# First two channel tiles of a GLU projected from unnormalized rows, the RMSNorm factor applied to their results

## The chip, the cores and the metric

The program runs on one core of a Trainium2 chip. The metric is the device time of one execution in microseconds. A core has a matrix engine (TensorE, here PE, with its weight loads PEld), a vector engine (VectorE, DVE), a scalar engine (ScalarE, ACT), a general one (GpSimd, POOL) and an engine that here only issues transfers (SyncE, SP). Each executes its own instructions strictly in order and waits on semaphores for the others.

## The reference, cut

One inference step of a streaming encoder: a Conformer convolution module, a SwiGLU feed-forward layer, a shared key and value projection, an attention layer with another feed-forward, a final norm. The change lies in the first projection of the convolution module.

```python
def rms_norm(x, g):
    xf = x.astype(jnp.float32)
    y = xf * lax.rsqrt(jnp.mean(xf * xf, axis=-1, keepdims=True) + EPS)
    return (y * g.astype(jnp.float32)).astype(x.dtype)

def conv_module(h, hist, g, w_pw1, b_pw1, w_dw, b_dw, ln_g, ln_b, w_pw2, b_pw2):
    a, gate = jnp.split(rms_norm(h, g) @ w_pw1 + b_pw1, 2, axis=-1)
    glu = a * jax.nn.sigmoid(gate)
    full = jnp.concatenate([hist.astype(glu.dtype), glu], axis=1)
    y = lax.conv_general_dilated(
        full, w_dw[:, None, :].astype(full.dtype), window_strides=(1,), padding="VALID",
        dimension_numbers=("NWC", "WIO", "NWC"), feature_group_count=D_MODEL) + b_dw
    y = jax.nn.silu(layer_norm(y, ln_g, ln_b))
    return h + y @ w_pw2 + b_pw2, full[:, -CONV_HIST:]
```

The model width is 1024; there are 512 prompt rows and 8 x 16 sample rows, 640 in all. Everything is float32.

## The kernel before

Channels lie on the 128 partitions, rows (frames) on the free axis, so the width is 8 slices k of 128 channels. The 640 rows are two halves g of 320 columns: half 0 has the 128 sample rows and 192 prompt rows, half 1 the other 320 prompt rows. `h` holds x of all rows.

**Exact products.** A float32 matmul is made of three cheaper ones: each operand is split into a high part and a remainder, x into `xh` and `xl`, a weight tile `raw` into `whi` and `wlo`, and `mm3` (L199) adds whi·xh, wlo·xh and whi·xl (L202, L203, L204) into one PSUM buffer. The high part is a copy on ACT to a rounding type (L178 for weights, L190 for rows), the remainder a subtraction on DVE (L183, L192). A weight tile of one channel tile c is 128 x 2048: both sides of the GLU (value and gate), 8 slices each. Two of `raw`, `whi` and `wlo` exist at a time; a third must wait for the first one's last use.

**The norm.** `rms` (L298) squares the 8 slices of a half (ACT L211, some DVE L214), adds the squares (L233), sums over the partitions with three small matmuls against a constant (L243), adds epsilon (`rst`, L280), takes the power -0.5 on POOL (L287), and spreads the result over the partitions with three matmuls (L257), so that the factor of each row lies in PSUM. Then for each slice DVE computes n = h · gain · factor (L309), ACT xh and DVE xl.

**The GLU.** `glu(c, g)` multiplies half g with weight tile c: 2 sides x 8 slices x 3 = 48 matmuls of 320 columns into two PSUM buffers out of four. ACT turns them into tanh (L814) and a scaled copy (L817), DVE multiplies these into `gall` (the gate: L823 for sample rows, L830 for prompt rows).

**The depthwise convolution** has 31 taps. They are shared out: DVE accumulates some channel tiles in PSUM (L866 starts one, L869 adds a tap, 512 prompt columns or 128 sample columns); POOL accumulates the prompt rows of c=0 and c=3 (`conv_pool`: ACT scales a shifted view into one of four buffers `cvt`, L876, POOL adds it to `ca`, L879); PE does the others with small diagonal matrices `w4` (L923), which POOL builds (`conv_load`, L890) from the tap weights `dwv`; three w4 buffers exist. All tiles end in `y` (L838), on which a LayerNorm follows, whose sums are again matmuls (L243).

**The order.** `PLAN` lists the steps: a c is glu(c, 0), b c is glu(c, 1), x is glu(1, 0) with the norm of half 1 put between its two sides (argument `mid`), y loads half 1 of x, later letters do further tiles and the convolution. A scheduling layer orders the instructions of each engine by priority: work in a `high_priority` block goes ahead of what was written earlier, `behind` and `issue_after` tie an instruction behind a given one. Transfers go through SP's queue in the order in which they are written: half 0 of x, weight tiles 0 and 1 in quarters, history, half 1 of x; ACT's queue takes the small vectors and `dwv`. While nothing is there to multiply, PE multiplies the identity (`warm`, L149), 30, 9 and 5 times at three places.

Half 1's norm borrows two w4 buffers for its first n (argument `hold`), so the second and third w4 are built after those n are used up.

Of the kernel before, what the change touches and what calls it, by code (L numbers as in the profile page):

```python
# [47 lines left out]
PL1 = (0, 2, 0, 0, 0, 0, 0, 0)  # L48
# [7 lines left out]
SSQ = 'avavavaa'  # L56
# [29 lines left out]
def tile_trunk(ctx, tc, xT, vecs, hist, w_pw1, w_pw2, w_in0, w_out0, w_os0, w_in1, w_out1, w_os1,  # L86
# [65 lines left out]
    def wsplit(src, k, n, parts=1, pool=0, cuts=1, gains=None, late=False, ties=()):  # L152
        raw = wp.tile([P, 2048], F32, tag="raw", name=nm("raw"))
# [18 lines left out]
        def split():  # L172
            with tc.high_priority(offset=HP):
                for i in range(cuts):
# [5 lines left out]
                    for eng, a, b in ((nc.vector, a, c), (nc.gpsimd, c, b)):  # L180
                        if a < b:
                            with behind(*tie):
                                eng.tensor_tensor(out=lo[:, a:b], in0=raw[:, a:b],  # L183
                                                  in1=hi[:, a:b].bitcast(F32), op=ALU.subtract)
# [37 lines left out]
    def colmean(st, pieces, n, cut, tag, eng=nc.gpsimd, accp=None, late=(KT, None)):  # L222
# [17 lines left out]
        for k, f in enumerate(srcs):  # L240
            s = f()
            for t, a in enumerate(tiles(n)):
                mean_end[0] = nc.tensor.matmul(st[:, 512 + t * w + k:513 + t * w + k], s[:, a:a + P],  # L243
                                               onec, start=True, stop=True).ins
# [53 lines left out]
    def rms(g, gain, engs=SQ, cut=CUT, eng=nc.gpsimd, hold=None, hook=None):  # L298
        n = gr[g][1]
        bc, _ = rstd_bc([hp(g, k) for k in range(KT)], n, engs, cut, None, eng,  # L300
                        accp=hold and hold(), hook=hook)
# [4 lines left out]
        for k in range(KT):
            t = hold() if hold and k < 2 else tp.tile([P, tw[0]], F32, tag="n1", name=nm("n1"),
                                                       bufs=NB1)
            norm_end["n"].append(nc.vector.scalar_tensor_tensor(  # L309
                out=t[:, :n], in0=hp(g, k), scalar=col(gain, k), in1=bc, op0=ALU.mult,  # L310
                op1=ALU.mult).ins)
# [458 lines left out]
    def first():  # L770
        with behind(mean_end[0]):
            warm(WARM[1])
        pws[0] = wsplit(w_pw1[0], 16, P, cuts=4, pool=PL1[0],
                        ties=[(norm_end["sq"], norm_end[e]) for e in ("acc", "acc", "rst", "rst")])

    with tc.issue_after(warm(WARM[0])), tc.high_priority(offset=2 * HP):
        xs = [rms(0, V_NCONV, SSQ, SCUT, nc.vector, hook=first), None]
    pws[1] = wsplit(w_pw1[1], 16, P, cuts=4, pool=PL1[1],
                    ties=(norm_end["sq"], norm_end["n"][3], norm_end["pow"]))
# [13 lines left out]

    def glu_(c, g, wh, wl, mid):
        n = gr[g][1]
        ps = []
        for ab in range(2):
            pt = mmt()
            def some(ks):
                return mm3(pt[:, :n], [(wh[:, (ab * 8 + k) * P:(ab * 8 + k + 1) * P],  # L800
                                        wl[:, (ab * 8 + k) * P:(ab * 8 + k + 1) * P])
                                       for k in ks], xk(xs[g], ks), ks[0] == 0, ks[-1] == KT - 1)

            if mid and ab:
                mid(lambda: some(range(0, 4)).ins)
                with tc.issue_after(norm_spread[0]):
                    some(range(4, KT))
            else:
                some(range(KT))
            ps.append(pt[:, :n])  # L810
        with tc.high_priority(offset=HP):
            cover.clear()
            t = tp.tile([P, tw[0]], F32, tag="t1", name=nm("t1"))
            glu_end[0] = nc.scalar.activation(out=t[:, :n], in_=ps[1], func=AF.Tanh, scale=0.5,  # L814
                                              bias=hb1[:, KT + c:KT + c + 1]).ins
            a = tp.tile([P, tw[0]], F32, tag="t2", name=nm("t2"))
# [1060 lines left out]
```

## Time and profile before

| | |
|---|---|
| median of 3 runs | 1432.19 us (1431.23 to 1434.5) |
| profiled execution | 1431.78 us |
| its span in the trace | 1430.0 us |
| granted TensorE clock | 1.000 |
| busy: PE, DVE, ACT, POOL | 99%, 78%, 52%, 19% of the span |

The profile is of one execution; its time is 1.78 us over its span, since what lies around the span is not in the trace. Times in the trace count from the span's start. A row of the timeline has start, length, engine, line, operation, output and inputs (buffer numbers left out), a count of equal instructions that follow each other, and, in brackets, how long the engine had been idle and what released it. A row of the groups has line, engine, operation, shape and count, then the busy time in us and the mean of one in ns, then the idle time before them. A row of the stretches has the stretch, its length, and for each engine the busy time and count, then the granted clock, the share of the transfer engines and GB/s.

### The profile page before, as it was taken

How to read it: one execution, taken by the hardware profiler on the slowest of the kernel's cores; microseconds unless marked ns; L12 is line 12 of the kernel's file. 1: busy time of each engine (PE TensorE's matmuls, PEld its weight loads, DVE VectorE, ACT ScalarE, POOL GpSimd, SP SyncE). 2: the span in 40 equal slices, each digit the busy share in tenths (PEclk: the TensorE clock that was granted, in tenths of full speed). 3: DMA queues.
4: the chain of work that ended last, by engine and by line, in shares of the span. 5: the costliest groups of instructions: out<-in, count | busy, mean ns of one | idle time of the engine just before them, and what ended most of it. 6: DMA issues, size and time to landing. Idle time of an engine off the chain costs nothing.

```text
span 1430.0 us, 28700 instructions
## 1 busy us (share of the span) xinstructions
PE 1416.8 (99%) x11076; PEld 1364.0 (95%) x11076; DVE 1113.5 (78%) x2490; ACT 746.9 (52%) x1633; POOL 278.4 (19%) x335
## 2 busy tenths in 40 slices
PE   9999999999999999999999999999999999999998
PEld 9998799999999999999998998888999999999998
DVE  7799867898888888765666757667898798798765
ACT  5666554554653554545654554544564564464453
POOL 5699121011111110112111111110011111111101
PEclk9999999999999999999999999999999999999999
DMA  7267424154644644524456555561244544554522
GB/s 248 91 176 187 123 84 143 32 122 122 169 107 121 148 115 117 139 89 174 165 185 205 187 179 173 181 218 51 60 108 118 147 125 110 145 131 109 135 72 74
DMA packets 93722, 192.62 MB, mean 135 GB/s; under 512 B 15121, under 2 KB 45585, under 8 KB 90129
## 3 DMA queue, kind: packets, MB, share of 16 engines
q1 hardware_dynamic: 79216, 160.59, 36.0%
q0 software_dynamic: 13504, 29.37, 10.5%
q8 instruction: 87, 1.43, 0.4%
q10 hardware_dynamic: 864, 0.83, 0.2%
q14 instruction: 51, 0.41, 0.1%
HBM read 179.14 MB, written 11.61 MB: 133 GB/s over the span
## 4 chain that ended last, share of the span: by engine, by line
PE 93%; DVE 4%; ACT 1%; issue 1%; DMA 1%; POOL 0%; DVEq 0%; ACTq 0%; POOLq 0%
PE mm L451 52%; PE mm L1311 11%; PE mm L202 6%; PE mm L204 6%; PE mm L203 6%; PE mm L923 3%; PE w L1311 2%; PE am L1484 1%; PE am L1556 1%; PE am L1500 1%; PE w L1455 1%; PE w L1518 1%; PE w L243 1%; PE mm L149 1%; PE w L257 1%
## 5 line engine op out<-in xcount | busy, mean ns | idle before, releaser
L451 PE MATMUL mm<-XH,whi 128*128 128x320 f32 x896 | 275.9, 310 | 1.0 <-ACT t L463 0.7
L451 PE MATMUL mm<-XH,wlo 128*128 128x320 f32 x896 | 276.2, 309 | 0.0
L451 PE MATMUL mm<-XL,whi 128*128 128x320 f32 x896 | 274.7, 309 | 0.0
L375 ACT ACTIVATE whi<-raw 128x512 fp32r<-128x512 f32 (+2 forms) x280 | 167.5, 613 | 148.4 <-PE mm L451 91.9
L376 DVE TENSOR_TENSOR wlo<-raw,whi 128x512 fp32r<-128x512 f32 (+2 forms) x280 | 183.8, 667 | 29.8 <-ACT whi L375 29.2
L451 PE MATMUL mm<-hid,whi 128*128 128x320 f32 x732 | 170.9, 310 | 0.0
L451 PEld LDWEIGHTS mm<-XH,whi 128*128 128x128 f32 x896 | 167.7, 188 | 2.8 <-ACT t L463 1.5
L451 PEld LDWEIGHTS mm<-XH,wlo 128*128 128x128 f32 x896 | 168.2, 188 | 0.0
L451 PEld LDWEIGHTS mm<-XL,whi 128*128 128x128 f32 x896 | 167.7, 188 | 0.0
L202 PE MATMUL mm<-xh,whi 128*128 128x320 f32 (+2 forms) x416 | 128.8, 312 | 0.5 <-DVE h L733 0.4
L203 PE MATMUL mm<-xh,wlo 128*128 128x320 f32 (+2 forms) x416 | 128.0, 309 | 0.0
L204 PE MATMUL mm<-xl,whi 128*128 128x320 f32 (+2 forms) x416 | 125.5, 310 | 1.0 <-DVE xl L192 1.0
L451 PEld LDWEIGHTS mm<-hid,whi 128*128 128x128 f32 x732 | 124.8, 188 | 1.5 <-DVE h L602 0.9
L451 PE MATMUL mm<-hid,wlo 128*128 128x320 f32 x366 | 113.0, 309 | 0.0
L451 PE MATMUL mm<-XH,shi 128*128 128x320 f32 x344 | 106.2, 310 | 1.2 <-DVE h L1588 0.7
L451 PE MATMUL mm<-XH,slo 128*128 128x320 f32 x344 | 106.0, 308 | 0.0
L602 DVE TENSOR_TENSOR h<-h,mm 128x320 f32<-128x320 f32 x168 | 79.1, 482 | 34.2 <-PE mm L451 34.2
L451 PE MATMUL mm<-XL,shi 128*128 128x320 f32 x344 | 105.6, 308 | 0.0
L375 ACT ACTIVATE shi<-raw 128x512 fp32r<-128x512 f32 (+1 forms) x114 | 66.4, 588 | 59.6 <-PE mm L451 31.6
L879 POOL TENSOR_TENSOR ca<-ca,cvt 128x512 f32<-128x512 f32 x60 | 89.5, 1492 | 17.3 <-ACT cvt L876 11.1
L428 POOL DMA_DIRECT2D s<-in_w_in x38 | 22.0, 578 | 309.1 <-ACT shi L375 67.3
L376 DVE TENSOR_TENSOR slo<-raw,shi 128x512 fp32r<-128x512 f32 (+1 forms) x114 | 72.0, 636 | 12.4 <-ACT shi L375 12.0
(337 smaller groups left out, 3663.1 us busy)
## 6 DMA issues: line engine op xcount, KB each, us to landing
raw<-in_w_in SPq DMA_DIRECT2D x152, 256.0 KB
s<-in_w_in POOLq DMA_DIRECT2D x76, 256.0 KB, 4.3
raw<-in_w_os SPq DMA_DIRECT2D x96, 192.0 KB
cache<-in_ck SPq DMA_DIRECT2D x32, 512.0 KB
cache<-in_cv SPq DMA_DIRECT2D x32, 512.0 KB
raw<-in_w_pw SPq DMA_DIRECT2D x11, 1024.0 KB
s<-in_w_os POOLq DMA_DIRECT2D x48, 192.0 KB, 3.6
raw<-in_w_kq SPq DMA_DIRECT2D x8, 1024.0 KB
```

The costliest lines, as they stand in the source:

```text
L149: end = nc.tensor.matmul(pt[:, 0:P], ident, ident, start=True, stop=True)
L202: nc.tensor.matmul(ps, wh, xh, start=(first and i == 0), stop=False)
L203: nc.tensor.matmul(ps, wl, xh, start=False, stop=False)
L204: end = nc.tensor.matmul(ps, wh, xl, start=False, stop=(stop and i == last))
L375: put_end[1] = nc.scalar.activation(out=hi, in_=src, func=AF.Copy).ins
L376: put_end[0] = nc.vector.tensor_tensor(out=lo, in0=src, in1=hi.bitcast(F32), op=sub).ins
L428: nc.gpsimd.dma_start(s1, src[:, 2 * n:3 * n])
L451: last = nc.tensor.matmul(pt, wt, v, start=(first and k == i == 0), stop=(k == n - 1 and i == 2), skip_group_check=True)
L602: hadd[i, u] = [nc.vector.tensor_tensor(out=hv, in0=hv, in1=pt, op=sub if row else add).ins]
L879: nc.gpsimd.tensor_tensor(out=acc, in0=acc, in1=pr, op=ALU.add)
L923: conv_end[0] = nc.tensor.matmul(pt[32 * q:32 * q + 32, 0:n], w4[0:r, 4 * tg + q, :], mv, start=(tg == 0), stop=(tg == 7)).ins
L1311: step_end[0] = nc.tensor.matmul(ps, w, x, start=i == j == 0, stop=i == len(wts) - 1 and j == 2).ins
```

## The change

The first two channel tiles, c=0 and c=1, are projected from rows that carry the gain but not the norm's factor; since that factor belongs to a row and not to a channel, it can be multiplied onto the 320 columns of the projection's result. The other six tiles use the normalized rows as before, which overwrite the raw ones in the same buffers.

- New function `rows`: for each slice, ACT makes xh = h · gain (rounded), DVE xl = h · gain - xh. It stands for both halves, before any norm.
- `half_rstd` computes the factor as before, and ACT copies it from PSUM to an SBUF tile `bc`, kept in `bch[g]`.
- In `glu_`, for c < 2, DVE multiplies each of the two PSUM results with `bch[g]` into the tiles t1 and t2 before ACT takes tanh and copy from there. These evictions are held back (list `evicts`) until the factor of their half exists.
- `rescale` makes n, xh and xl of all 8 slices again, n now with `bch[g]` from SBUF, into the same `xh`, `xl`.
- The loads interleave x and the quarters of the first weight tile (`ARRIVE`), then the second weight tile, half 1 of x, and `dwv`, which moves from ACT's queue to SP's.
- All squares are taken on ACT (three were on DVE), all remainders of weight tile 1 on DVE (POOL had four pieces of 256 columns).
- The first 30 warm-up products become 19, the other two places have none.
- The order of the plan: glu(0,0), then glu(1,0) with half 0's norm between (x), glu(0,1) with half 1's norm between (z), the rescale of half 0 (r0), glu(1,1), the rescale of half 1 (r1). Within c < 2 the products go by half of the slices, so that they can start with slices 0 to 3.
- The w4 builds are tied behind the latest power; ACT's conversions for POOL's taps of c=0 are tied, two rows apart, behind the xh of the rescale.

```diff
+AT = 2, 2
+ARRIVE = "x0 x1 w0 w2 x2 x3 w1 w3".split()
...
-PL1 = (0, 2, 0, 0, 0, 0, 0, 0)
+PL1 = (0, 0, 0, 0, 0, 0, 0, 0)
...
-SSQ = 'avavavaa'
+SSQ = 'aaaaaaaa'
...
-WARM = 30, 9, 5, 0
+WARM = 19
...
-PLAN = ("a0 y x1 b0 b1 q0 dp1s0 c2 ds1p2 D3 C4 S3 q3 C5 E6 u S4 A4 F6 u k ds2 B4 E7 e S5 A5 F7 f k k k S6 A6 "
+PLAN = ("a0 x1 z0 r0 b1 r1 q0 dp1s0 c2 ds1p2 D3 C4 S3 q3 C5 E6 u S4 A4 F6 u k ds2 B4 E7 e S5 A5 F7 f k k k S6 A6 "
...
+    def rows(g, gain, ks, x):
+        for k in ks:
+            with tc.high_priority(offset=HP):
+                nc.scalar.activation(out=x[0][:, k, :], in_=hp(g, k), func=AF.Copy,
+                                     scale=col(gain, k))
+                nc.vector.scalar_tensor_tensor(out=x[1][:, k, :], in0=hp(g, k),
+                                               scalar=col(gain, k),
+                                               in1=x[0][:, k, :].bitcast(F32), op0=ALU.mult,
+                                               op1=ALU.subtract)
+
+    def half_rstd(g, engs, eng, hook, late=(KT, None)):
         n = gr[g][1]
...
+        b = xp.tile([P, n], F32, tag=f"bc{g}", name=nm("bc"))
+        with tc.high_priority(offset=HP):
+            nc.scalar.activation(out=b, in_=bc, func=AF.Copy)
+        return b
+
+    def rescale(g, gain, x):
+        n = gr[g][1]
         for k in range(KT):
...
+            t = tp.tile([P, tw[0]], F32, tag=sqt[0], name=nm("n"))
+            nc.vector.scalar_tensor_tensor(out=t[:, :n], in0=hp(g, k), scalar=col(gain, k),
+                                           in1=bch[g], op0=ALU.mult, op1=ALU.mult)
+            norm_end["rows"] = xsplit(t[:, :n], x[0][:, k, :], x[1][:, k, :]).ins
...
+        if c < 2:
+            parts = [(ab, range(4 * u, 4 * u + 4)) for u in range(2) for ab in range(2)]
+        else:
+            parts = [(ab, range(KT)) for ab in range(2)]
...
+                if c < 2:
+                    av, bv = a[:, :n], t[:, :n]
+                    nc.vector.tensor_tensor(out=av, in0=pts[0], in1=bch[g], op=ALU.mult)
+                    nc.vector.tensor_tensor(out=bv, in0=pts[1], in1=bch[g], op=ALU.mult)
...
+            with behind(*(norm_end["xh"][min(2 * j - 9, -1):][:1] if j > 1 and c == 0 else ())):
+                nc.scalar.activation(out=pr, in_=taps(c, 1, j), func=AF.Identity, scale=wj,
+                                     **({} if j else {"bias": col(V_BDW, c)}))
...
     def conv_load(c):
         w4 = w4t().rearrange("p (a b) -> p a b", a=32)
...
+        with behind(norm_end["pow"]):
...
-            pws[c + 1] = wsplit(w_pw1[c + 1], 16, P)
+            pws[c + 1] = wsplit(w_pw1[c + 1], 16, P, ties=(norm_end["rows"], norm_end["xh"][-1]))
...
+            if g == 0:
+                glu(1, 0, *pws[1], mid=(AT[0], mid))
+                rows(1, V_NCONV, range(KT), xs[1])
+            else:
+                glu(0, 1, *pws[0], mid=(AT[1], mid))
+                pws[2] = wsplit(w_pw1[2], 16, P, pool=PL1[2], cuts=2)
+        elif op == "r":
+            with tc.high_priority(offset=HP * c), behind(*[norm_end["lo"]][:c]):
+                rescale(c, V_NCONV, xs[c])
```

Two places on DVE's queue matter. The first is what follows the `rst` of half 1 (a row has line, operation, output and inputs with their numbers, and shape). Before, two gates and the rows of half 1, whose factor is `w_39` in PSUM:

```order
L280 TENSOR_SCALAR rst_373<-w_39_346 128x3
L823 SCALAR_TENSOR_TENSOR gall<-t_34_308,t_35_310 128x8x16
L830 SCALAR_TENSOR_TENSOR gall<-t_34_308,t_35_310 128x192
L309 SCALAR_TENSOR_TENSOR w_52_394<-h,vec,w_39_346 128x320
L309 SCALAR_TENSOR_TENSOR w_53_398<-h,vec,w_39_346 128x320
L309 SCALAR_TENSOR_TENSOR n_54_402<-h,vec,w_39_346 128x320
L309 SCALAR_TENSOR_TENSOR n_55_406<-h,vec,w_39_346 128x320
L192 TENSOR_TENSOR xl_393<-w_52_394,xh_392 128x320
```

Now it is the second half of half 0's rescale, with its factor `bc_305` in SBUF; then the evictions of glu(0, 1) with half 1's factor `bc_426`, and the remainder of c=2's weight tile:

```order
L292 TENSOR_SCALAR rst_407<-w_35_379 128x3
L203 TENSOR_TENSOR xl_112<-n_468,xh_111 128x320
L333 SCALAR_TENSOR_TENSOR n_476<-h,vec,bc_305 128x320
L203 TENSOR_TENSOR xl_112<-n_472,xh_111 128x320
L333 SCALAR_TENSOR_TENSOR n_480<-h,vec,bc_305 128x320
L203 TENSOR_TENSOR xl_112<-n_476,xh_111 128x320
L333 SCALAR_TENSOR_TENSOR n_484<-h,vec,bc_305 128x320
L203 TENSOR_TENSOR xl_112<-n_480,xh_111 128x320
L203 TENSOR_TENSOR xl_112<-n_484,xh_111 128x320
L862 TENSOR_TENSOR t_49_441<-mm_353,bc_426 128x320
L863 TENSOR_TENSOR t_48_440<-mm_354,bc_426 128x320
L193 TENSOR_TENSOR wlo_449<-raw_447,whi_448 128x1024 x2
```

So the rows stand behind the `rst` of the other half, and POOL's power and its three w4 builds, which follow on POOL's queue, run beside them.

The second place is ahead of the remainder of c=3's weight tile (2048 columns in one piece). Before, DVE went from c=2's remainder over a gate and the first taps to it:

```order
L183 TENSOR_TENSOR wlo_714<-raw_712,whi_713 128x1024 x2
L830 SCALAR_TENSOR_TENSOR gall<-t_68_550,t_69_552 128x320
L866 TENSOR_SCALAR w_101_649<-gall,dwv,vec 128x512
L866 TENSOR_SCALAR w_116_840<-gall,dwv,vec 128x128
L866 TENSOR_SCALAR w_101_649<-gall,dwv,vec 128x128
L183 TENSOR_TENSOR wlo_723<-raw_721,whi_722 128x2048
```

Now 30 rows stand between the two remainders: the evictions of glu(1, 1), two gates, the rescale of half 1, and taps between its rows. The last of them:

```order
L333 SCALAR_TENSOR_TENSOR n_569<-h,vec,bc_426 128x320
L203 TENSOR_TENSOR xl_114<-n_565,xh_113 128x320
L918 SCALAR_TENSOR_TENSOR w_104_671<-gall,dwv,w_104_671 128x512
L333 SCALAR_TENSOR_TENSOR n_573<-h,vec,bc_426 128x320
L203 TENSOR_TENSOR xl_114<-n_569,xh_113 128x320
L918 SCALAR_TENSOR_TENSOR w_104_671<-gall,dwv,w_104_671 128x128
L203 TENSOR_TENSOR xl_114<-n_573,xh_113 128x320
L918 SCALAR_TENSOR_TENSOR w_104_671<-gall,dwv,w_104_671 128x512
L918 SCALAR_TENSOR_TENSOR w_104_671<-gall,dwv,w_104_671 128x128
L918 SCALAR_TENSOR_TENSOR w_104_671<-gall,dwv,w_104_671 128x512
L193 TENSOR_TENSOR wlo_736<-raw_734,whi_735 128x2048
```

The same rows on ACT and POOL follow: the conversions for POOL's taps of c=0 stand one after every second xh of that rescale.

More of the change, by code (lines that the diff above doesn't have):

```diff
@@ L150, in warm, with wsplit @@
         return end.ins
-    def wsplit(src, k, n, parts=1, pool=0, cuts=1, gains=None, late=False, ties=()):
-        raw = wp.tile([P, 2048], F32, tag="raw", name=nm("raw"))
+    def wsplit(src, k, n, parts=1, pool=0, cuts=1, gains=None, late=False, ties=(), raw=None, order=None):
+        loaded = raw is not None
+        raw = raw or wp.tile([P, 2048], F32, tag="raw", name=nm("raw"))
         hi = wp.tile([P, 2048], F32R, tag="whi", name=nm("whi"))
@@ L156, in wsplit @@
         sz = k * n
-        if parts > 1:
+        if loaded:
+            pass
+        elif parts > 1:
             nc.sync.dma_start(raw[:, :sz].rearrange("p (m c) -> p m c", m=parts), src)
@@ L162, in wsplit @@
                 a, b = sz * i // cuts, sz * (i + 1) // cuts
-                with behind(norm_end["x"]) if cuts > 2 else nullcontext():
-                    nc.sync.dma_start(raw[:, a:b], src[:, a:b])
+                nc.sync.dma_start(raw[:, a:b], src[:, a:b])
         if gains is not None:
@@ L171, in wsplit, with split @@
             return hi, lo
-        def split():
+        def split(only=None):
             with tc.high_priority(offset=HP):
-                for i in range(cuts):
+                for i in range(cuts) if only is None else (only,):
                     a, b = sz * i // cuts, sz * (i + 1) // cuts
@@ L242, in colmean @@
             for t, a in enumerate(tiles(n)):
-                mean_end[0] = nc.tensor.matmul(st[:, 512 + t * w + k:513 + t * w + k], s[:, a:a + P],
-                                               onec, start=True, stop=True).ins
+                with behind(*sum_cover):
+                    mean_end[0] = nc.tensor.matmul(st[:, 512 + t * w + k:513 + t * w + k],
+                                                   s[:, a:a + P], onec, start=True, stop=True).ins
         r = tp.tile([P, 4], F32, tag=tag, name=nm(tag))
@@ L768, in tile_trunk @@
     pws = {}
[L770 to L779, printed above, removed]
+    xs, bch, evicts = [new_xs(0), new_xs(1)], [None, None], []
+    with tc.issue_after(warm(WARM)):
+        split0 = wsplit(None, 16, P, cuts=4, pool=PL1[0], late=True, raw=raw0)
+        for piece in ARRIVE:
+            i = int(piece[1])
+            if piece[0] == "x":
+                rows(0, V_NCONV, (2 * i, 2 * i + 1), xs[0])
+            else:
+                pws[0] = split0(i)
+                if i == 2:
+                    early_lo = norm_end["lo"]
+    pws[1] = wsplit(w_pw1[1], 16, P, cuts=4, pool=PL1[1])
+    load_x(1)
+    nc.sync.dma_start(dwv, vecs[:, V_N:])
     load_hist(0, 2)
-    nc.scalar.dma_start(dwv, vecs[:, V_N:])
     def w4t():
@@ L791, in glu, with store, flush @@
         if g == 0:
-            nc.sync.dma_start(convs_out[:, c], gs[:, c])
+            def store():
+                nc.sync.dma_start(convs_out[:, c], gs[:, c])
+            evicts.append(store)
+            flush(g)
+    def flush(g):
+        while bch[g] is not None and evicts:
+            evicts.pop(0)()
     def glu_(c, g, wh, wl, mid):
         n = gr[g][1]
[L796 to L816, printed above, removed]
-            nc.scalar.activation(out=a[:, :n], in_=ps[0], func=AF.Identity, scale=0.5,
-                                 bias=hb1[:, c:c + 1])
-            ns = 0 if g else NB * SB
-            tie = [norm_end["n"][9]] if mid else []
-            if g == 0:
-                with behind(*tie):
+        pts = [mmt()[:, :n], mmt()[:, :n]]
```

97 lines of the change are left out of this document (61 added, 36 removed).

## The prediction

> **What bounds the kernel now.** I read the page first.
>
> ```profile
> PE 1416.8 (99%) x11076; PEld 1364.0 (95%) x11076; DVE 1113.5 (78%) x2490; ACT 746.9 (52%) x1633; POOL 278.4 (19%) x335
> ...
> PE 93%; DVE 4%; ACT 1%; issue 1%; DMA 1%; POOL 0%; DVEq 0%; ACTq 0%; POOLq 0%
> ```
>
> PE carries 93% of the chain that ended last, so the time moves only by what PE waits for or stops executing. The changed program is the same as the old one from the end of the conv module on (the engines' orders differ in their first quarter alone), so I need one thing: when PE reaches the LayerNorm of the conv module. Next come stretches of the start.
>
> ```profile
> core 0: us, PE busy (x) PEld busy (x) DVE busy (x) ACT busy (x) POOL busy (x), PEclk, DMA share, GB/s
> ...
> 30.00:40.00 10.00, 9.54 (x66) 9.24 (x65) 9.50 (x15) 3.09 (x7) 5.13 (x3) 1.00 0.25 97
> 40.00:60.00 20.00, 20.00 (x138) 20.00 (x137) 14.47 (x23) 15.30 (x24) 12.36 (x8) 1.00 0.33 115
> 60.00:80.00 20.00, 20.00 (x139) 20.00 (x138) 16.79 (x32) 13.57 (x20) 18.98 (x14) 1.00 0.38 110
> ```
>
> From 40 us on PE is full; DVE has 5.5 and 3.2 us of room in 40 to 80, and POOL hardly any after 60. Now PE's timeline, where the milestones are.
>
> ```profile
> 1.64 8.95 PE L149 MATMUL mm<-ident 128*128 128x128 f32 x60 [1.64 <-POOL ident masks.py:199]
> ...
> 15.07 0.41 PE L202 MATMUL mm<-xh,whi 128*128 128x320 f32 x1
> ...
> 46.82 0.46 PE L202 MATMUL mm<-xh,whi 128*128 128x320 f32 x2
> ...
> 60.90 0.31 PE L202 MATMUL mm<-xh,whi 128*128 128x320 f32 x1
> ...
> 156.93 0.83 PE L243 MATMUL w<-onec,acc 128*128 128x1 f32 x6
> ```
>
> The first real product starts at 15.07; until then PE multiplies the identity. Tile c=2 begins at 46.82 and c=3 at 60.90: 96 matmuls in 14.08 us, 0.147 each. The LayerNorm sums start at 156.93. These are the marks against which I put the change.
>
> **The head.** The loads set the first product.
>
> ```profile
> 5.98 0.47 ACT L211 ACTIVATE sq<-h 128x320 f32<-128x320 f32 x1 [1.23 <-DMA h<-in_xa]
> ...
> 11.82 2.67 ACT L178 ACTIVATE whi<-raw 128x512 fp32r<-128x512 f32 x4 [0.29 <-DMA raw<-in_w_pw]
> ```
>
> ACT is released at about 5.9 by the second x piece, at 11.8 by the first quarter of the second weight. Between lie two x pieces (0.33 MB each) and five weight quarters (0.26 MB): 1.97 MB in 5.9 us, 0.33 MB/us. In the new order x0, x1, w0, w2 the second weight quarter is there by about 7.5 instead of after four x pieces. Splitting a quarter costs 0.62 on ACT and 0.68 on DVE (groups below), so PE gets its first three products by **8.4** (7.8 to 9.2), 6.7 us earlier. The shorter warm-up (19 for 30) ends before that, so it removes nothing from the sum. On SP's queue half 1's x now stands behind both weights as before, and the load of dwv (taken from ACT's queue) behind that x: 4.7 MB from 4.2 us on at that rate is about 18, and its first readers, the w4 and the taps, come after 33; cost nothing.
>
> Now the durations for all that follows, one row per shape over the first 160 us.
>
> ```profile
> L183 DVE TENSOR_TENSOR wlo<-raw,whi 128x512 fp32r<-128x512 f32 x4 | 2.6, 684 | 0.0
> ...
> L183 DVE TENSOR_TENSOR wlo<-raw,whi 128x1024 fp32r<-128x1024 f32 x2 | 2.4, 1221 | 0.5 <-ACT whi L178 0.5
> ...
> L178 ACT ACTIVATE whi<-raw 128x512 fp32r<-128x512 f32 x8 | 4.7, 621 | 0.4 <-DMA raw<-in_w_pw 0.3
> ...
> L178 ACT ACTIVATE whi<-raw 128x1024 fp32r<-128x1024 f32 x2 | 2.0, 1052 | 0.0
> ...
> L192 DVE TENSOR_TENSOR xl<-n,xh 128x320 fp32r<-128x320 f32 x14 | 10.6, 782 | 0.4
> ...
> L309 DVE SCALAR_TENSOR_TENSOR n<-h,vec,w 128x320 f32<-128x320 f32 x14 | 7.0, 538 | 1.4 <-PE w L257 1.4
> ...
> L869 DVE SCALAR_TENSOR_TENSOR w<-gall,dwv,w 128x512 f32<-128x512 f32 x60 | 42.7, 745 | 0.2
> L869 DVE SCALAR_TENSOR_TENSOR w<-gall,dwv,w 128x128 f32<-128x128 f32 x90 | 29.4, 348 | 1.1
> ...
> L817 ACT ACTIVATE t<-mm,hb 128x320 f32<-128x320 f32 x16 | 8.3, 517 | 6.6 <-PE mm L204 6.6
> ...
> L866 DVE TENSOR_SCALAR w<-gall,dwv,vec 128x512 f32<-128x512 f32 x2 | 1.6, 807 | 0.1
> ...
> L287 POOL TENSOR_TENSOR rst<-rst,mhalf 128x3 f32<-128x3 f32 x2 | 2.1, 1072 | 10.4 <-DVE rst L280 10.4
> ```
>
> Back to back, an operation starts before the one ahead of it ends:
>
> ```profile
> 32.26 0.89 DVE L192 TENSOR_TENSOR xl<-w,xh 128x320 fp32r<-128x320 f32 x2
> ...
> 37.79 0.99 DVE L309 SCALAR_TENSOR_TENSOR n<-h,vec,w 128x320 f32<-128x320 f32 x2
> ```
>
> Two xl take 0.89 and two n 0.99, where one alone takes 0.48 and 0.54; each further one costs 0.40 and 0.46. I use such steps: 0.40 xl and the new evictions (two-tensor multiply with an input in PSUM, not in this trace; bounded by 0.40 and the n's 0.46), 0.46 n and the raw rows' xl (same kind of instruction), 0.70 and 0.30 for a tap of 512 and 128, 0.72 and 0.32 for L866, 0.44 for a gate.
>
> **What the change adds** on DVE: 8 evictions (3.2), 16 raw xl (7.4), four 256-column pieces taken from POOL (2.1), less three squares (1.5): 11.2 us. ACT gets 16 raw xh, 3 squares, 2 factor copies, about 9 us, and waits more than it works here. Neither is free, since DVE's room is 5.5 us in 40 to 60. So I follow DVE's order, as the order lists show it.
>
> Half 0's norm: ahead of its rst stand 8 raw xl, 8 weight quarters, 7 adds of squares and all 8 raw xl of half 1 (about 14.5 us from 5.5 on), so rst is at 20, or at 21 with the waits for squares, the power on POOL 1.07 behind it, and PE idles about 1 us before the spread. Products of both tiles' half 0 end at 24.9. Then DVE: four evictions, four gates, five n and three xl (6.3 us, and 1 for adds of squares on POOL beside them) to rst of half 1 at **31.8**, where PE's half-1 sums (31.0 to 31.5) arrive too.
>
> **Where POOL holds DVE.** Behind that power come three w4 builds, now tied to it, while DVE has five xl and three n left.
>
> ```profile
> 29.00 1.91 POOL L890 TENSOR_TENSOR w<-i,dwv 128x1024 f32<-128x1024 f32 x1
> 32.83 4.22 POOL L890 TENSOR_TENSOR w<-i,dwv 128x1024 f32<-128x1024 f32 x2 [1.91 <-DVE xl L192]
> 47.09 48.05 POOL L879 TENSOR_TENSOR ca<-ca,cvt 128x512 f32<-128x512 f32 x30 [10.04 <-ACT cvt L876]
> ...
> 30.42 1.01 DVE L309 SCALAR_TENSOR_TENSOR w<-h,vec,w 128x320 f32<-128x320 f32 x2 [1.85 <-PE w L257]
> ...
> 33.07 2.21 DVE L192 TENSOR_TENSOR xl<-n,xh 128x320 fp32r<-128x320 f32 x1
> 35.19 2.00 DVE L823 SCALAR_TENSOR_TENSOR gall<-t,t 128x128 f32<-128x128 f32 x1
> ...
> 56.38 4.68 DVE L869 SCALAR_TENSOR_TENSOR w<-gall,dwv,w 128x512 f32<-128x512 f32 x8
> ```
>
> Beside a w4, an xl took 2.21 instead of 0.48 and a gate 2.00, each until the w4 ended; both read two tensors from SBUF. The n beside the first w4 (its factor in PSUM) kept its 0.5, and so did the taps (their sum in PSUM): eight took 4.68 within POOL's 30 adds. The n of the rescale reads h and the factor, now copied to SBUF: no row has it. Its bounds are the taps, which share its form (free), and the gate, which shares the places of its operands (held); what parts the held rows from the free ones is the places, so I take it as held. The Trainium skill, page "SBUF — State Buffer", section "SBUF: two separate sides", says that a DVE operation with two SBUF inputs and a GpSimd operation that reads SBUF lock each other out for a whole instruction. These rows agree with it; by it the sum is this forecast, by the taps' row alone it is rival B1.
>
> So: xl, n and xl slip in before the first w4 starts at about 33.05; then one DVE operation passes after each w4, n until 35.4, xl until 37.6, n until 39.85, and the last two xl end at 40.7, or 41.9 with rst 0.6 later and one operation fewer ahead: **41.1** (with nothing held 36.6). Eviction 41.5, its pass on ACT 41.9, whi of c=2 in two pieces to 43.9, wlo 42.9 to 45.3. PE has run out at 40, waits, and runs c=2 effectively from **43.9**, 2.9 earlier than before, to 58.0.
>
> **Where the rest goes.** From 45.3 DVE must do, ahead of c=3's wlo: 2 evictions 0.8, 2 gates 0.9, 8 n 3.7, 8 xl 3.2, three of L866's kind 1.4, taps 4 x 0.7 and 3 x 0.3: 13.7 us. Three POOL adds of 1.3 fall between the rows, each holding one operation for none to all of it (0 to 3.9): I take 1.8. That gives 60.8, and wlo of 2048 columns
>
> ```profile
> L183 DVE TENSOR_TENSOR wlo<-raw,whi 128x2048 fp32r<-128x2048 f32 x7 | 20.2, 2892 | 0.0
> ```
>
> (2.4 with no add against it, 2.9 on average) ends at **63.4**. PE, ready at 58.0, waits 5.3 us; c=3 runs as if from 63.3, **2.4 later** than its mark. In before's order this wlo stands ahead of the taps and there are no rows to rescale by then: it ended at 54.9.
>
> ```profile
> 51.66 3.22 DVE L183 TENSOR_TENSOR wlo<-raw,whi 128x2048 fp32r<-128x2048 f32 x1
> ```
>
> **The POOL chain.** It is late too: three adds lie between rows, and the fourth waits on ACT behind whi of c=3 and then for wlo, to end at 64.7. Before, the add that waited for this wlo was the fifth and ended at 56.0 (the 51.66 and 3.22 above, and an add): with one add more to do, the chain is 10 us late. What that meets:
>
> ```profile
> 138.94 8.90 POOL L879 TENSOR_TENSOR ca<-ca,cvt 128x512 f32<-128x512 f32 x5 [1.09 <-ACT cvt L876]
> ...
> 150.49 0.74 ACT L838 ACTIVATE y<-ca 128x192 f32<-128x192 f32 x2
> ```
>
> The chain ended at 147.84; 10 us on, less the gap of 1.09, it ends at 156.8. Two copies (0.74) and two adds of sums (0.5 each) later come the LayerNorm's sums: 158.6, while PE, 2.4 late, gets there at 159.3. The evictions that stand behind conversions on ACT have three or four conversions fewer ahead than before, 4 to 5.5 us of the 10. Neither is over the edge; for the handovers I add 0.5.
>
> **Sum**, against the profiled run of 1431.78: +2.4 at c=3, +0.5 up to the LayerNorm: **1434.7**. (The median of the runs shown is 0.41 above that run.) The head's 6.7 us come back as two waits of PE, of about 4 and 5.3.
>
> **Rivals.** *B, not slower: less is held.* If n isn't held, DVE is free of the rescale at 39.65, and the adds cost 0.7 less: c=3 as if from 61.1, **1432.3** (B1). If in addition the w4 fall behind the xl, DVE is done at 36.6 and c=2's whi is bound by PE's last use of its buffer at about 39: wlo ends at 42.4 instead of 45.3, and without the adds' 1.8 c=3 starts at 58.6: **1429.4** (B2). For it: 0.5 us in rst decides which operations meet a w4, and the taps are unhurt. Against: three w4 in 5.7 us meet eight operations in 3.5 nearly whatever their phase; and 13.7 us of rows stay, so the 6.7 can't be reached.
>
> *D, slower: the POOL chain sets the LayerNorm or an eviction.* From 10.7 us late on, each us of the chain is PE's. One more conversion behind whi is 1.4, one more wlo against an add 1.9; at 13 us it is 2.3 more: **1437.0**. For it: POOL has 1 us of room in 60 to 80. Against: the conversions moved.
>
> *E, the head isn't gained.* PE's half-1 sums at 31 to 31.5 lie just ahead of rst, so each us by which the first product comes after 9 delays rst, the w4 and all behind them. At 10.5: **1436.2**.
>
> **How the numbers follow.** Chances: forecast 0.38, B1 0.17, B2 0.20, D 0.15, E 0.10. Two times within 0.2% (2.9 us) can't be told apart here; the edges are 1429.3 and 1435.1. The forecast's own bounds (rst 0.6, the adds' 0 to 3.9, wlo 0.5, the 0.5) are 1432.5 to 1437.3, so 0.17 of it lies above the edge; with D and nearly all of E slower has 0.41. Faster has 0.14 of B2 and 0.03 of B1; the rest, 0.42, is within. The range 1429.0 to 1438.4 leaves out the best of B2 and D with E.
>
> **What to look for.** A first product at about 8.4 (E if after 9.5); three w4 beside n and xl of the rescale, each held about 2 us (B if n stay at 0.5); PE waiting near 40 to 44 and 58 to 63 for wlo, c=3's wlo ending near 63.4; the POOL chain 10 us late, and the sums at about 159.4, behind the xa products, not behind the copies of POOL's result (D). A PE that waits nowhere between 25 and 63 would show the forecast wrong altogether.

## The result, and the profile after

The changed kernel takes 1439.32 us, the median of 6 runs (1439.05 to 1442.16), beside 1432.08 for the kernel before (6 runs, 1431.23 to 1434.5): 7.24 us more, a ratio of 1.0055 [1.0042, 1.0068]. That lies above the range. The profiled execution is one of two of the six near 1442 (1442.16, span 1440.4): it is 7.3 us behind the kernel before at 1120 us and 10.4 at its end, 3.1 more, of which 1.8 arise at one wait of PE near 1249 us for a weight tile that landed late, and the times of the other four show nothing of this. Up to the LayerNorm its marks can be read as they stand.

The page after, busy time by engine and the chain that ended last:

```profile
PE 1416.5 (98%) x11026; PEld 1361.3 (95%) x11026; DVE 1127.1 (78%) x2511; ACT 755.0 (52%) x1654; POOL 277.4 (19%) x331
...
PE 83%; DVE 6%; POOL 5%; ACT 2%; DMA 2%; issue 1%; POOLq 0%; DVEq 0%; ACTq 0%
```

PE is busy as long as before (1416.5 for 1416.8), although some 6 us of warm-up work are gone (6.4 where there were 12.5): other work takes that much longer, 2.7 us of it at half clock (last section). The growth of the span itself is waiting. In the chain PE's share falls from 93 to 83%, and POOL's rises from 0 to 5%. The same stretches as before:

```profile
core 0: us, PE busy (x) PEld busy (x) DVE busy (x) ACT busy (x) POOL busy (x), PEclk, DMA share, GB/s
30.00:40.00 10.00, 10.00 (x73) 10.00 (x72) 9.82 (x12) 2.36 (x5) 7.33 (x4) 1.00 0.09 31
40.00:60.00 20.00, 16.96 (x95) 16.33 (x94) 18.56 (x38) 13.17 (x23) 4.14 (x3) 0.83 0.16 53
60.00:80.00 20.00, 19.05 (x130) 18.79 (x129) 18.76 (x32) 13.89 (x22) 18.05 (x12) 1.00 0.41 136
```

From 40 to 60 POOL works 4.1 us, where it worked 12.4: that is the work that will be late. PE has lost 3 us there, and its granted clock is down to 0.83. PE's timeline, at the marks used before:

```profile
8.05 0.93 PE L213 MATMUL mm<-xh,whi 128*128 128x320 f32 x2
...
43.35 0.63 PE L213 MATMUL mm<-xh,whi 128*128 128x320 f32 x1 [2.72 <-ACT whi L188]
...
62.32 0.42 PE L214 MATMUL mm<-xh,wlo 128*128 128x320 f32 x1 [0.94 <-DVE wlo L193]
...
90.38 1.96 PE L975 MATMUL mm<-xa,w 128*32 128x128 f32 x64
...
107.96 0.42 PE L213 MATMUL mm<-xh,whi 128*128 128x320 f32 x1 [1.04 <-ACT t L866]
...
121.36 0.41 PE L213 MATMUL mm<-xh,whi 128*128 128x320 f32 x1 [1.40 <-ACT t L866]
...
163.11 0.83 PE L255 MATMUL w<-onec,acc 128*128 128x1 f32 x6
```

and of before the one mark that was not shown, the first product of the convolution (called "first xa" from here on):

```profile
89.15 1.96 PE L923 MATMUL mm<-xa,w 128*32 128x128 f32 x64
```

| mark on PE | before | after | later by |
|---|---|---|---|
| first real product | 15.07 | 8.05 | -7.0 |
| c=3, as if run without a wait | 60.90 | 62.17 | 1.3 |
| first xa | 89.15 | 90.38 | 1.2 |
| LayerNorm sums | 156.93 | 163.11 | 6.2 |

(62.17 is the 62.32 of the first wlo product less one product of 0.147; it stands to about 0.15.) So 7 us are gained at the head, and some 8 are given back at the two places of the forecast, but not in its sizes. Before c=2 PE stands 3.0 us, where about 4 were forecast; then it runs at half clock to 50 us, which costs 2.7 and was not forecast; and at 62 it waits 0.94 instead of 5.3, which would have been about 3.6 without the half clock. But 4.95 us more are lost between the first xa and the sums, where the kernel before has no wait at all. What PE waits for there:

```profile
engine line waited for: us in total, times, longest us
PE mm L213 <- ACT t L866: 2.4, 2, 1.4
PE mm L975 <- ACT y L887: 0.8, 1, 0.8
PE mm L975 <- issue: 0.5, 1, 0.5
PE mm L213 <- ACT t L864: 0.2, 1, 0.2
```

These add up to 3.9 of the 4.95 us; the rest lies beside the same stops, where the next products come up to 0.1 us later than their pace. ACT is named, and ACT has room. The reason stands one row above each eviction on ACT's timeline:

```profile
106.77 0.72 ACT L926 ACTIVATE cvt<-gall,dwv 128x512 f32<-128x512 f32 x1 [3.92 <-POOL ca L929]
107.40 0.51 ACT L866 ACTIVATE t<-mm,hb 128x320 f32<-128x320 f32 x1
...
120.17 0.72 ACT L926 ACTIVATE cvt<-gall,dwv 128x512 f32<-128x512 f32 x1 [0.77 <-POOL ca L929]
120.80 0.51 ACT L866 ACTIVATE t<-mm,hb 128x320 f32<-128x320 f32 x1
...
141.81 0.72 ACT L926 ACTIVATE cvt<-gall,dwv 128x512 f32<-128x512 f32 x1 [0.64 <-POOL ca L929]
142.44 0.51 ACT L887 ACTIVATE y<-mm,vec 128x320 f32<-128x320 f32 x1
```

A conversion for POOL's taps waits until POOL has read one of the four `cvt` buffers; the eviction that PE needs stands right behind it on ACT. And POOL is late:

```profile
61.09 40.39 POOL L929 TENSOR_TENSOR ca<-ca,cvt 128x512 f32<-128x512 f32 x25 [4.30 <-ACT cvt L926]
101.44 4.03 POOL L941 TENSOR_TENSOR w<-i,dwv 128x1024 f32<-128x1024 f32 x1
105.44 2.65 POOL L929 TENSOR_TENSOR ca<-ca,cvt 128x512 f32<-128x512 f32 x2
```

The chain that ended last goes the same way. From 63 us up to the rows below it is POOL's adds, with the wait for a w4 and a few short pieces of ACT between them, and behind the last row it is PE's products up to the sums, with one stop of 0.46:

```profile
140.49 1.29 POOL ca L929
141.81 0.72 ACT cvt L926
142.53 0.42 ACT y L887
143.00 2.81 PE mm L975 x64
```

POOL's 30 adds for c=0 end at 108.1, before at 95.1 (47.09 and 48.05): 13 us later. About 9 of these exist already at the fifth add; the other 4.03 are a w4 build, held by a wlo of DVE, that now stands ahead of the last two adds.

### The profile page after: what moved, and what is told of

Same layout as the page of the kernel before. It is cut to its first block, busy times and chain, and to the rows that moved or that the text cites. A ratio compares the mean times of both kernels' runs of the same rounds, so it can differ in the third digit from the quotient of the medians.

```text
span 1440.4 us, 28651 instructions
## 1 busy us (share of the span) xinstructions
PE 1416.5 (98%) x11026; PEld 1361.3 (95%) x11026; DVE 1127.1 (78%) x2511; ACT 755.0 (52%) x1654; POOL 277.4 (19%) x331
## 4 chain that ended last, share of the span: by engine, by line
PE 83%; DVE 6%; POOL 5%; ACT 2%; DMA 2%; issue 1%; POOLq 0%; DVEq 0%; ACTq 0%
PE mm L473 50%; PE mm L1375 10%; POOL ca L929 5%; PE mm L213 4%; PE mm L214 4%; PE mm L215 4%; PE w L1375 2%; PE mm L975 2%; DMA raw<-in_w_in 1%; PE am L1548 1%; PE am L1620 1%; PE am L1564 1%; PE w L1519 1%; PE w L1582 1%; DVE n L333 1%
## 5 line engine op out<-in xcount | busy, mean ns | idle before, releaser
L398 DVE TENSOR_TENSOR wlo<-raw,whi 128x512 fp32r<-128x512 f32 (+2 forms) x280 | 184.0, 668 | 32.2 <-ACT whi L397 31.5
L473 PE MATMUL mm<-XL,shi 128*128 128x320 f32 x344 | 105.6, 308 | 0.0
L397 ACT ACTIVATE shi<-raw 128x512 fp32r<-128x512 f32 (+1 forms) x114 | 66.3, 588 | 61.8 <-PE mm L473 31.9
L213 PEld LDWEIGHTS mm<-xh,whi 128*128 128x128 f32 x416 | 79.1, 191 | 9.8 <-ACT whi L188 4.7
```

What stands on the lines that cost most here:

```text
L213: nc.tensor.matmul(ps, wh, xh, start=(first and i == 0), stop=False)
L397: put_end[1] = nc.scalar.activation(out=hi, in_=src, func=AF.Copy).ins
L398: put_end[0] = nc.vector.tensor_tensor(out=lo, in0=src, in1=hi.bitcast(F32), op=sub).ins
L473: last = nc.tensor.matmul(pt, wt, v, start=(first and k == i == 0), stop=(k == n - 1 and i == 2), skip_group_check=True)
```

## The experiments

Each kernel was timed beside the kernel before on one chip; the medians of the kernel before were 1431.47 (the first four), 1431.31 (the next four) and 1431.17 (the last two). Line numbers shift by one to three where lines were added.

**The factor from PSUM.** Does the place of the factor hold the rows?

```diff
-                                           in1=bch[g], op0=ALU.mult, op1=ALU.mult)
+                                           in1=bcp[g], op0=ALU.mult, op1=ALU.mult)
```

(`bcp[g]` is the PSUM tile from which `bch[g]` is copied.)

> The rescale's n reads the norm's factor from PSUM, as the kernel before does, instead of from the SBUF copy; nothing else. Theory A (POOL's w4 builds hold a DVE operation when both its inputs lie in SBUF): n beside a w4 takes 0.54 instead of 2.09, only xl are held; the rescale of half 0 ends at about 39.7 instead of 41.4, c=3's wlo at about 60 instead of 62.3, LayerNorm sums about 2 earlier, 1437 us. Rival B (holding goes by the form of the instruction or by POOL alone): n stays at 2.1 beside a w4, nothing moves, 1439.3 us.

Measured: 1436.65, ratio 1.0042 [1.0026, 1.0058]. DVE's timeline beside the three w4, first of the changed kernel, then of this one:

```profile
33.94 2.09 DVE L333 SCALAR_TENSOR_TENSOR n<-h,vec,bc 128x320 f32<-128x320 f32 x1
35.95 2.20 DVE L203 TENSOR_TENSOR xl<-n,xh 128x320 fp32r<-128x320 f32 x1
38.19 2.09 DVE L333 SCALAR_TENSOR_TENSOR n<-h,vec,bc 128x320 f32<-128x320 f32 x1
```

```profile
33.91 0.55 DVE L334 SCALAR_TENSOR_TENSOR n<-h,vec,w 128x320 f32<-128x320 f32 x1
34.37 1.62 DVE L203 TENSOR_TENSOR xl<-n,xh 128x320 fp32r<-128x320 f32 x1
36.03 0.55 DVE L334 SCALAR_TENSOR_TENSOR n<-h,vec,w 128x320 f32<-128x320 f32 x1
```

The same operation at the same place takes 0.55 instead of 2.09 when its factor lies in PSUM. That settles it for the n. It frees little at once, because the w4 then meet xl instead. Still, the remainder of c=3's weight tile ends 2.7 earlier (59.55 for 62.26), and the sums come at 159.61.

**Fewer taps on POOL.** Is it POOL's chain that PE waits for after 90? This kernel leaves out the last 7 of the 30 adds of c=0 on POOL, so the rows of c=0 lack 7 of their 31 taps.

```diff
-        ends = POOLED if c else (W,)
+        ends = POOLED if c else (24,)
```

> Leaves out the last 7 of the 30 additions that POOL makes for c=0's prompt rows (so those rows lack 7 of 31 taps). Theory C (between c=3 and the LayerNorm the loss grows from 1.3 to 6.2 us because ACT's conversions wait for POOL and the evictions stand behind them): POOL's c=0 chain ends about 10 us earlier, PE's waits for ACT's t near 108 and 121 go, the sums come at about 158.5 instead of 163.1, 1434.5 us. Rival D (the growth is DVE's full queue of taps, or PE's own work): the waits stay, sums at 162 to 163, 1438 to 1439 us.

Measured: 1437.69, 1.0044 [1.0029, 1.0059]. The chain ends at 94.37, and PE's two waits at 107.96 and 121.36 (2.4 us) are gone; one of 0.48 near 97 is left of its kind. But the sums come at 161.57 only: DVE's own taps, not shortened by this edit, end at 155.6, and a copy of their result is next:

```profile
155.61 0.28 ACT L887 ACTIVATE y<-w 128x128 f32<-128x128 f32 x1 [1.44 <-DVE w L918]
```

So those two waits are POOL's, and behind them DVE's taps are late as well. With POOL's chain out of the way the sums come only 1.5 us earlier: DVE's taps are a second limit close behind the first. Part of their lateness in the changed kernel has the same root, since there DVE waits 1.49 us at 111.28 for an eviction of ACT that stands behind a conversion. The total is a miss.

**Conversions not tied to the rows.** The other way round: POOL's adds may start early and fall between the rows.

```diff
-            with behind(*(norm_end["xh"][min(2 * j - 9, -1):][:1] if j > 1 and c == 0 else ())):
+            with nullcontext():
```

> Takes away the ties that put c=0's conversions for POOL between the rows of half 1's rescale. Theory A: POOL's adds then stand close together from 49 on and each lets one DVE operation of the rescale pass, so 16 row operations take 1.4 each; c=3's wlo ends at 66 to 69 instead of 62.3, PE waits that much longer, and POOL's chain gains 4 to 6 us: 1440 to 1443 us. Rival (the adds hold little, as the three adds between rows cost 0.4 each): wlo at 63, POOL's chain 5 us earlier, 1435 us.

Measured: 1441.07, 1.0071 [1.0056, 1.0086]. From 52.8 us on the adds meet rows of the rescale and hold eight of them; the first two adds, from 49.46, hold none:

```profile
52.80 1.33 DVE L203 TENSOR_TENSOR xl<-n,xh 128x320 fp32r<-128x320 f32 x1
54.05 1.58 DVE L333 SCALAR_TENSOR_TENSOR n<-h,vec,bc 128x320 f32<-128x320 f32 x1
...
66.57 2.28 DVE L193 TENSOR_TENSOR wlo<-raw,whi 128x2048 fp32r<-128x2048 f32 x1
```

The remainder ends at 68.85, the first xa is at 96.68, and from there to the sums (164.40) PE waits nowhere: 67.72 us, as before (67.78). POOL's chain ends at 101.87, only 5.2 behind the first xa. So with a chain early enough against PE's mark the whole growth of 4.95 is gone. This does not move the chain alone: PE's own mark is 6.3 us later here, which gives DVE and ACT as much more room. Without the ties the sums come 1.3 us later than with them (164.40 for 163.11); the two ratios are too close to tell whether the ties also save time in the whole.

**The w4 after three adds.** The three w4 leave the first rescale.

```diff
+                if c == 0 and j == 3:
+                    norm_end["ca"] = e
...
-        with behind(norm_end["pow"]):
+        with behind(norm_end["ca"]):
```

(`e` is POOL's add.)

> The first three w4 builds are tied behind POOL's third add of c=0 instead of behind the power of half 1's norm. Theory A: nothing is held in the rescale of half 0, its last xl ends at about 37 instead of 41.4, PE's wait before c=2 shrinks to under 1.5 us, c=2's wlo ends at about 42.5 to 43 instead of 45.7; the w4 now meet c=3's wlo (held up to 5 us), which ends at 60 to 62, and POOL's chain is 1 to 3 later: 1438 to 1440 us. Rival (the w4 aren't what delays the rescale): last xl still after 40, 1441 us or more because of the later chain.

Measured: 1439.41, 1.0059 [1.0044, 1.0074]. The first rescale ends at 36.74 instead of 41.36, but the w4, now at 53.9 to 60.3, hold rows of the second, and a remainder that starts late and beside adds takes 3.4. PE waits 3.71 for it:

```profile
63.71 0.64 PE L214 MATMUL mm<-xh,wlo 128*128 128x320 f32 x1 [3.71 <-DVE wlo L193]
```

The w4 cost about the same in either place.

**The last three n of half 0 in w4 buffers.** As in the kernel before, a w4 can then not be built until its buffer's n is used up.

```diff
+        own = {} if g else {k: w4t() for k in (7, 6, 5)}
...
-            t = tp.tile([P, tw[0]], F32, tag=sqt[0], name=nm("n"))
+            t = own.get(k) or tp.tile([P, tw[0]], F32, tag=sqt[0], name=nm("n"))
```

> The last three n of half 0's rescale are written to the three w4 buffers, so that the w4 builds can't start before those rows are split; the place on POOL's queue stays. Theory A: n and xl of half 0's rescale take 0.5 each after rst, its last xl ends at 36.7 to 37.2 (41.4), the builds run from about 37 to 43 beside DVE's wait for whi and one piece of c=2's wlo; that wlo ends at 43 to 44 (45.7), PE waits 1 to 2 us before c=2 and keeps its clock, c=3's wlo ends at 60 (62.3), and the sums come about 3 earlier than 163.1 with fewer waits for evictions: 1436 us. Rival (the builds only move the holding on to wlo and evictions): wlo of c=2 still at 45 or later, 1439 us.

Measured: 1436.01, 1.0031 [1.0019, 1.0043]. The first rescale ends at 37.28, the remainder of c=3 at 59.73, the sums are at 159.85. It is 4.70 us over the kernel before, where the changed kernel is 7.24 and the one with the factor from PSUM 5.18.

**Both together.** The factor from PSUM and the n in w4 buffers.

> e5 and the factor of the rescale from PSUM (e1) together. Theory A: as e5, and the n of half 1's rescale aren't held by POOL's adds: c=3's wlo ends at 58.5 to 59.5, POOL's fourth add starts at about 58, sums at 157.5 to 159, 1433.5 us. Rival (with the builds away the factor's place is worth nothing): as e5, 1436 us.

Measured: 1433.07, 1.0011 [1.0001, 1.0020]; remainder at 58.37, first xa at 88.02, sums at 157.98. The gains add up roughly: 1.76 us over the kernel before are left of 7.24, 5.5 less, where the two alone take off 2.1 and 2.5; at the sums it is 5.1 less, where the two alone take off 3.5 and 3.3. PE is now 1.1 us ahead of before at the first xa, and still 1.05 late at the sums.

**Then the weight tile of c=3 in two halves,** tied behind the last xh of the second rescale, or behind its third last:

```diff
-            pws[c + 1] = wsplit(w_pw1[c + 1], 16, P, ties=(norm_end["rows"], norm_end["xh"][-1]))
+            pws[c + 1] = wsplit(w_pw1[c + 1], 16, P, cuts=2, ties=(norm_end["xh"][-1],))
```

> e6, and c=3's weight tile is split in two pieces, its tie left to half 1's last xh alone. Theory A: whi's first half is there 0.95 earlier and DVE takes it before the last taps, so the wlo that PE needs first ends at about 57.5, 1.5 ahead of e6, and PE waits under 1 us for c=3; sums at 156.5 to 158, 1432.5 us. Rival (c=3 isn't what sets the sums by now; POOL's chain is): PE's waits move to the evictions and y copies, 1434 us.

> e7 with the tie two xh earlier: c=3's weight is split ahead of the last two slices of half 1's rescale. Theory A (DVE's rows and wlo form one queue, whose sum sets c=3): PE gets wlo about 3 earlier than in e6 but waits for the last xl inside c=2; c=3 starts at about 57 to 58 all the same, 1432 to 1433 us; ACT's conversions come sooner and POOL's chain gains 1 to 2. Rival: the waits inside c=2 cost more than they save, 1434 to 1435 us.

Measured: 1433.69, 1.0017 [1.0008, 1.0027], and 1433.14, 1.0011 [1.0001, 1.0020]. In the first of them PE's first xa is at 85.04, 4.1 us ahead of before, and nothing of it is left at the sums (158.37). The view of waits between 90 and 165:

```profile
PE mm L978 <- ACT y L890: 4.9, 3, 2.7
```

That is the plainest answer of the series: PE 3 us earlier than with both edits alone, the sums 0.4 us later. PE's own progress no longer sets them. In the second PE is as early (84.99), POOL's chain ends 1.3 earlier than in the first, and the sums come 1.6 earlier (156.78).

**POOL's adds earlier, on top of that.** The ties one row apart instead of two, or three rows for every two conversions:

```diff
-            with behind(*(norm_end["xh"][min(2 * j - 9, -1):][:1] if j > 1 and c == 0 else ())):
+            with behind(*(norm_end["xh"][min(j - 9, -1):][:1] if j > 1 and c == 0 else ())):
```

(in the second kernel `(3 * j) // 2 - 9`; the rest as in the kernel with the tie to the last xh)

> e7 with POOL's conversions of c=0 one row apart instead of two, so that seven adds fall into half 1's rescale instead of three. Theory C (in e7 POOL's chain, 4 adds behind the kernel before, sets the y copies and the sums, while c=3 has 4 us in hand): add 8 starts at about 60, the last add of c=0 ends 4 us earlier than e7's 104.2, c=3's first wlo ends at 59.5 to 60.5 instead of 56.8, PE's waits for y at 133 to 155 fall from 4.9 to under 2, sums at 155.5 to 157, 1430.5 to 1431.5 us, level with the kernel before or just under. Rival (each add costs the rescale as much as it gains the chain): c=3's wlo at 63, sums at 158 or later, 1433 to 1434 us.

> e7 with the conversions one and a half rows apart, five adds within the rescale. Theory C: between e7 and e9: last add of c=0 2 us earlier than e7's, wlo of c=3 at 58 to 59, waits for y about 3, sums at 156.5 to 157.5, 1431.5 to 1432.5 us. Rival: 1433 to 1434 us.

Measured, in 5 rounds: 1432.26, 1.0008 [0.9999, 1.0017], and 1431.70, 1.0005 [0.9996, 1.0014]. Both are level with the kernel before; none of the ten beats it. PE's first xa in the one and in the other:

```profile
88.80 1.96 PE L978 MATMUL mm<-xa,w 128*32 128x128 f32 x64
```

```profile
86.10 1.96 PE L978 MATMUL mm<-xa,w 128*32 128x128 f32 x64
```

2.7 us apart; POOL's chain for c=0 ends at 101.97 and 102.00, and the sums are at 156.86 and 156.71. In the first the sums are where they were expected, but the total lies above the 1430.5 to 1431.5 expected; the second is as expected.

**All of them in one table,** in the order of the chain's end (us; the kernel with fewer taps, where DVE's taps end last, is left out):

| kernel | first xa | POOL's c=0 chain ends | sums | first xa + 67.8 | sums less chain's end |
|---|---|---|---|---|---|
| changed | 90.38 | 108.1 | 163.11 | 158.2 | 55.0 |
| w4 after adds | 93.77 | 108.1 | 162.87 | 161.6 | 54.8 |
| n in w4 buffers | 87.84 | 105.6 | 159.85 | 155.6 | 54.3 |
| factor from PSUM | 87.68 | 105.1 | 159.61 | 155.5 | 54.5 |
| split | 85.04 | 104.2 | 158.37 | 152.8 | 54.2 |
| both | 88.02 | 103.9 | 157.98 | 155.8 | 54.0 |
| split early | 84.99 | 102.9 | 156.78 | 152.8 | 53.8 |
| ties mixed | 86.10 | 102.0 | 156.71 | 153.9 | 54.7 |
| ties one apart | 88.80 | 102.0 | 156.86 | 156.6 | 54.9 |
| no ties | 96.68 | 101.9 | 164.40 | 164.5 | 62.5 |
| before | 89.15 | 95.1 | 156.93 | 156.9 | 61.8 |

The sums come at the later of two times: first xa + 67.8, or the chain's end + 54 to 55. In the last three rows PE sets them, and in these three alone PE has no wait there. In the other eight the first xa moves over 8.8 us and the last column over 1.2. The two meet when the chain ends about 13.4 us behind the first xa; the kernel before has 6.0, the changed one 17.7. The rule is read off these kernels, and the 13.4 is computed from it. The last steps of the way differ: with both edits and with the split, the last eviction that PE waits for stands behind the copies of POOL's result, and in the kernel with the early split PE's last stop (0.8) is put down to a transfer. And as the kernel with fewer taps shows, DVE's taps can set the sums too.

## Why the prediction was wrong

**The failed step** is in the paragraph on the POOL chain: "Neither is over the edge; for the handovers I add 0.5." Against +0.5 stand 4.95 us between the first xa and the sums. Two sizes in that step were off.

- *How late the chain is.* 10 us were counted up to the fifth add and taken over to the end. At the fifth add it was 9.0 (it ended at 65.0, against 56.0). The remaining 4.03 are the fourth w4: in the order before it stood behind the last add (95.09 to 97.26, next to a chain that ended at 95.14), now ahead of the last two, and a wlo on DVE doubled its length. The prediction says nothing of its place on POOL's queue. That the build is part of the 13 us is read from the timeline: in three kernels (the split, and the two with changed ties) it took 1.9 instead of 4.0, but in none was this the only difference.
- *Which way from the chain to the sums.* The step priced the result copies of c=3, and gave the chain 53.5 us from its end to the sums (158.6 less 105.1). The path that ended last runs over ACT's evictions behind conversions, and takes 55.0 in the changed kernel. "Three or four conversions fewer ahead" was right as a count, but how much room those evictions had was never worked out.

Together, 2.95 and 1.5 us, they make up the 4.5 by which the sums passed the 158.6 given for the chain. This is rival D, chance 0.15: its mechanism is what happened, by the eviction that it names second, and its price (2.3 more at 13 us) came from the copies and was too small.

**A term mis-sized the other way** is c=3: +2.4 foreseen, 1.3 measured. The remainder ended at 62.26, not 63.4.

```profile
53.17 0.93 DVE L333 SCALAR_TENSOR_TENSOR n<-h,vec,bc 128x320 f32<-128x320 f32 x1
...
56.21 0.93 DVE L333 SCALAR_TENSOR_TENSOR n<-h,vec,bc 128x320 f32<-128x320 f32 x1
...
59.98 2.28 DVE L193 TENSOR_TENSOR wlo<-raw,whi 128x2048 fp32r<-128x2048 f32 x1
```

Two n lost 0.4 each to POOL's adds between the rows, 0.8 where 1.8 was taken. By the table this term, too large or not, no longer mattered: the chain set the sums.

**What was right.** The first product at 8.05 (8.4). Half 1's rst at 32.37 (31.8 in the prediction, whose terms as written, 24.9 + 6.3 + 1, give 32.2). The n held by the w4 as xl are, 2.09 each: this was taken from the places of the operands against the taps' row, and the run with the factor in PSUM shows it. By the rule of the Trainium skill, page "SBUF — State Buffer", section "SBUF: two separate sides", a DVE operation with two SBUF inputs can be held by a GpSimd (POOL) operation that reads SBUF. The traces agree: with both inputs in SBUF the row took 2.09, with one in PSUM 0.55. The first rescale's end at 41.36 (41.1), c=2's remainder at 45.70 (45.3), and both waits of PE in their places, though not in their sizes (3.0 for about 4, and 0.94 for 5.3, with 2.7 us of half clock between them that the prediction does not have). B1 and B2 fall with the held n, E with the first product. The stated sign to watch, sums "behind the xa products, not behind the copies of POOL's result", did come out so, and was a poor sign: the xa products had themselves waited for POOL, over ACT.

**What stays open.** The time grew by 7.24 us and the sums by 6.18. The other 1.1 us come later: in the profiles of most of these kernels PE loses steps of up to about 1 us in the feed-forward layers (the changed kernel its first by 321 us), in code that the change leaves alone. In the level kernels, too, the sums are no later than before's while the medians are 0.5 and 1.1 over it. No run was spent on it.

## What to carry to other kernels

Where a change puts work ahead of a slow engine's chain, mark the end of that chain, not only the engine on the critical path: here PE was back within 1.2 us of its mark, and the loss came in the 70 us behind it, from a chain that had gone from 6 to 18 us behind PE. Read the whole queue of the slow engine up to that end, with the builds that stand between its pieces of the chain, and look on every in-order queue for what stands behind an instruction that waits for one of its buffers. And a factor copied from PSUM to SBUF can cost its reader more than the copy: in this trace 1.5 us for each row that met a w4.

## What the runs showed that was not expected

The granted clock of PE fell to one half after idle stretches of about 1.2 to 3 us, and not after others of the same length. Stretches of the changed kernel, with the columns as above (behind the five engines the granted clock, the transfers' share and GB/s):

```profile
40.00:44.00 4.00, 1.27 (x6) 0.66 (x4) 2.63 (x6) 3.00 (x5) 0.00 (x0) 0.90 0.00 0
44.00:48.00 4.00, 3.70 (x14) 3.67 (x15) 4.00 (x8) 2.51 (x7) 0.00 (x0) 0.50 0.36 78
48.00:52.00 4.00, 4.00 (x23) 4.00 (x23) 4.00 (x10) 2.72 (x5) 1.29 (x1) 0.75 0.44 184
```

and of the kernel with the factor from PSUM, at two places:

```profile
40.00:44.00 4.00, 1.93 (x9) 1.41 (x8) 2.82 (x5) 2.91 (x4) 0.00 (x0) 0.86 0.00 0
44.00:48.00 4.00, 4.00 (x22) 4.00 (x21) 4.00 (x10) 2.92 (x6) 0.00 (x0) 0.71 0.60 190
...
136.00:140.00 4.00, 1.32 (x50) 1.05 (x40) 3.96 (x11) 2.39 (x4) 3.76 (x4) 1.00 0.65 145
```

In the changed kernel PE is busy 1.27 of 4 us and then runs until about 50.0 at half clock: the 21 products from 44.30 to 50.08 stand 0.267 apart on most steps instead of 0.147 and take 2.7 us more, hidden here by the wait for c=3's remainder that followed. In the other kernel 2.1 idle us near 42 brought half clock until 46.3, about 1.5 us more, and 2.7 idle us at 136 to 140 brought none. The shortest idle time with half clock behind it is in the kernel with both edits, 1.24 us before 59.3.

Read at its edges, half clock lasts from 43.19 to 50.02 (6.8 us) in the changed kernel, from 42.87 to 46.29 (3.4) in the other, and from 57.93 to 68.17 (10.2) in the kernel with the w4 after three adds: one, two or three times 3.4. In the 3.41 us just ahead of the first two, changed kernel first, PE was partly busy:

```profile
39.78:43.19 3.41, 0.85 (x6) 0.59 (x5) 2.19 (x5) 2.19 (x4) 0.15 (x1) 1.00 0.00 0
39.46:42.87 3.41, 1.65 (x10) 1.16 (x8) 2.23 (x4) 2.19 (x3) 0.43 (x1) 1.00 0.00 0
```

In the kernel with both edits it was busy 2.17 us of such a stretch, and half clock followed; with the factor from PSUM it was busy 1.62 between 138.45 and 141.86, and none did. So no fixed share of busy time, taken over stretches laid out this way, decides it, and what does stays open. The Trainium skill, page "TensorE: Matmul & The Clock Gate", section "Part 1: The HAM clock gate (the "warmup" mystery)", gives a window of about 3.4 us that runs freely, and calls the effect run-variable. That two idles of like length fare differently agrees with a free window; that 1.2 to 2 idle us were enough does not agree with a whole idle window, and there the measurement decides.
